# Decoding the retrieved experts of four token tiles together, with a binary selection of sub-keys

## The chip, the cores and the metric

The kernel runs on one core of a Trainium2 chip. The metric is the device time of one execution in microseconds (us), less being better. An execution varies by some 0.1% around the median.

## The reference, cut to what matters

A first block (attention with forget gates, RWKV-7 time mixing, gated feed-forward) and a second one (HGRN2, retention, a PEER feed-forward over 16384 experts) run over 512 tokens of width 1024. The change lies in the retrieval of PEER: for each token and each of 8 heads, the best 16 of 128 sub-keys are taken in each of two halves, the best 16 of their 256 sums follow, and each winner's position is turned back into an expert's index.

```python
q = (ht @ w_q).reshape(T, 8, 2, 128)
s = jnp.einsum('thpd,hpkd->thpk', q, sub_keys)
top_s, top_i = lax.top_k(s, 16)
cand = top_s[:, :, 0, :, None] + top_s[:, :, 1, None, :]
cand_idx = top_i[:, :, 0, :, None] * 128 + top_i[:, :, 1, None, :]
best_s, best_c = lax.top_k(cand.reshape(T, 8, 256), 16)
expert_idx = jnp.take_along_axis(cand_idx.reshape(T, 8, 256), best_c, axis=-1)
gates = jax.nn.softmax(best_s, axis=-1)
# out[t] = sum over the 128 winners e of gate * gelu(u_e . h_t) * v_e
```

## The kernel before

All weights stream through one ring in a fixed order. A tile `raw` of 128x1024 is loaded on SP's queue, ACT rounds it to `hi` (L245), and VectorE or POOL subtracts to get `lo` (L248); three matmuls (L271 to L273) then make one product of nearly full precision. While `pool_split` is 1 (from the start of `peer` to the end of the gate stage), all these subtractions are POOL's. `next_w` keeps three splits and five loads ahead. A scheduler that simulates the program sets the order of each engine's instructions from program order and priorities; on the chip each engine then works strictly in that order.

`peer` (L1423) does the last part of the second block. Its stages:

1. `retrieve` (L1239). For each of four pairs of heads `hp` and each of four halves `c`: a product with a piece of `w_q` (24 matmuls, L1255), a copy `q` on ACT (L1257), four matmuls with the sub-keys, one for each tile of 128 tokens (`psc`, L1260), a copy `sc` on ACT (L1262), and `top16` for each tile on VectorE (L1230: maximum of 8, their index, replacement, maximum, index). After two halves, POOL adds the candidates: of the 16x16 sums only those 112 are formed that can win, 4x16 and 12x4 (L1271, L1274), and `top16` takes 16 of the 112.
2. `decode` (L1281), once for each pair of heads and each tile, so 16 times. It makes the gates by softmax (the exponential is ACT's, L1288), turns a position among the 112 into two numbers from 0 to 15 by shifts, masks, casts and a predicated copy (L1297 to L1311), compares each with 0 to 15 (`eq`, 32x16 elements, L1313, VectorE), multiplies with the sub-key indices `tif` (L1314, POOL) and sums (`sel`, L1315, VectorE). The tiles go in the order 3, 0, 1, 2 and have buffers of their own.
3. `slots_T` (L1352): transposes of `sel` and the gates of the tiles 0 to 2, and a copy `slT` on ACT.
4. `gate_matrix` (L1363), the gate stage: in 96 groups of four tokens, one-hot tiles `ohA` (VectorE, four instructions, L1375) and `ohB` (three groups of eight on POOL, L1379, the others on VectorE, L1381), their products `pg` (L1384), and a copy to `gstage` (L1386), which goes to memory as a dense matrix of gates.
5. `expert_act` (L1390): products of the tokens with expert rows `u`, 24 matmuls of 384 columns and a GELU each. 40 of them stand ahead of the main loop: 25 without a condition, then 12 tied to finished gate groups, then 3 behind the last group.
6. The main loop over 128 groups of experts (L1452): `wf`, its split, and the products with `v`. Tile 3 goes another way here: its rows are gathered one by one (`gather_rows`, L1317) during that loop.

## Time and profile before

| | us |
|---|---|
| median of three runs | 3087.77 |
| the three runs | 3086.38 to 3088.63 |
| the profiled execution | 3085.74 |
| its span, first to last instruction | 3084.0 |
| TensorE busy, share of the span | 96% |
| VectorE, ACT, POOL busy | 63%, 40%, 49% |
| mean granted clock of TensorE | 0.986 |

The span is what the profiler recorded of one execution on the core. PE is TensorE's matmul row, PEld its weight loads, DVE is VectorE, SP the queue of transfers. Matmuls are pipelined, and a busy PE is not PE at its peak. The busy share is a mean over stages with different limits, so a stage is read by itself. The clock is given as a share of full speed.

### The profile page before, as it was taken

The page shows a single profiled execution, that of the slowest core. Times are in us where ns is not written, and L with a number is a line of the kernel's source. Part 1 is how long each engine was busy: PE and PEld are TensorE (multiplying, and loading weights), DVE is VectorE, ACT ScalarE, POOL GpSimd, SP SyncE. Part 2 cuts the span into 40 slices and gives each one's busy share as a digit, 9 for nine tenths or more (in the row PEclk, how much of TensorE's full clock was granted, in tenths as well). Part 3 has the DMA queues.
Part 4 walks back from the last instruction along what each step waited for, and adds up shares of the span by engine and source line. Part 5 has one row for each costly group of instructions (what it writes and reads, how often), then busy time and mean ns, then how long its engine had stood idle before and what let it go on. Part 6 is the DMA issues. An engine that isn't in the chain of part 4 may idle for free.

```text
span 3084.0 us, 40810 instructions
## 1 busy us (share of the span) xinstructions
PE 2945.5 (96%) x15129; PEld 2542.2 (82%) x15129; DVE 1940.8 (63%) x3421; ACT 1229.7 (40%) x1925; POOL 1507.6 (49%) x1150
## 2 busy tenths in 40 slices
PE   7998998999999999999999987888999999999998
PEld 6877787888878878888888877887899999999877
DVE  4247655443134663455532699999677878777898
ACT  5455654222242443344422323466333333333333
POOL 3213213222235662233332447877677777767775
PEclk9998999999999999999999998999999999999999
DMA  4120013333332112322233322345888888898897
GB/s 158 57 66 10 1 38 105 97 96 96 96 110 82 59 45 82 99 85 82 82 119 117 120 62 77 116 174 195 287 302 308 298 312 297 305 317 297 314 324 254
DMA packets 174358, 473.64 MB, mean 154 GB/s; under 512 B 15056, under 2 KB 64592, under 8 KB 172624
## 3 DMA queue, kind: packets, MB, share of 16 engines
q1 hardware_dynamic: 137296, 336.80, 33.4%
q0 software_dynamic: 36864, 134.23, 12.3%
q8 instruction: 120, 1.97, 0.3%
q14 instruction: 78, 0.64, 0.1%
HBM read 439.49 MB, written 31.46 MB: 153 GB/s over the span
## 4 chain that ended last, share of the span: by engine, by line
PE 77%; DVE 13%; issue 4%; DMA 2%; ACT 2%; POOL 2%; SPq 0%; DVEq 0%; POOLq 0%; ACTq 0%
PE acc L272 14%; PE acc L271 14%; PE acc L273 14%; PE A L273 3%; PE A L272 3%; PE A L271 3%; PE B L272 3%; PE B L271 3%; PE B L273 3%; PE pg L1384 2%; DMA urow<-ev,ei 2%; PE i L811 2%; PE lev L988 1%; DVE wk L1235 1%; PE C L273 1%
## 5 line engine op out<-in xcount | busy, mean ns | idle before, releaser
L248 POOL TENSOR_TENSOR lo<-raw,hi 128x1024 fp32r<-128x1024 f32 x224 | 553.0, 2470 | 758.2 <-ACT hi L245 729.1
L271 PE MATMUL acc<-u,hi 128*128 128x512 f32 (+3 forms) x2344 | 859.1, 367 | 16.9 <-ACT eact L1399 7.2
L273 PE MATMUL acc<-u,lo 128*128 128x512 f32 (+3 forms) x2344 | 859.3, 367 | 16.3 <-POOL lo L248 16.3
L272 PE MATMUL acc<-u,hi 128*128 128x512 f32 (+3 forms) x2344 | 858.6, 366 | 0.2 <-DVE u L478 0.2
L245 ACT ACTIVATE hi<-raw 128x1024 fp32r<-128x1024 f32 x447 | 472.5, 1057 | 944.2 <-PE acc L272 496.2
L248 DVE TENSOR_TENSOR lo<-raw,hi 128x1024 fp32r<-128x1024 f32 x223 | 318.2, 1427 | 297.3 <-ACT hi L245 297.0
L271 PEld LDWEIGHTS acc<-u,hi 128*128 128x128 f32 (+1 forms) x2344 | 444.9, 190 | 72.5 <-ACT eact L1399 8.5
L273 PEld LDWEIGHTS acc<-u,lo 128*128 128x128 f32 (+1 forms) x2344 | 444.9, 190 | 67.7 <-POOL lo L248 18.6
L272 PEld LDWEIGHTS acc<-u,hi 128*128 128x128 f32 (+1 forms) x2344 | 445.2, 190 | 54.1 <-issue 2.7
L1339 DVE SCALAR_TENSOR_TENSOR urow<-urow,h4row 128x1024 f32<-128x1024 f32 x128 | 198.4, 1557 | 92.1 <-DMA urow<-eu,ei 91.5
L1349 DVE SCALAR_TENSOR_TENSOR po<-urow,act,po 128x1024 f32<-128x1024 f32 x127 | 193.9, 1527 | 66.4 <-DMA urow<-ev,ei 65.6
L1331 POOL DMA_INDIRECT urow<-eu,ei x128 | 189.6, 1481 | 34.7 <-issue 22.8
L1331 POOL DMA_INDIRECT urow<-ev,ei x128 | 175.6, 1372 | 44.6 <-DVE po L1349 18.4
L1410 ACT ACTIVATE wh<-wf 128x384 fp32r<-128x384 f32 x128 | 67.2, 526 | 313.8 <-PE D L272 268.7
L248 POOL TENSOR_TENSOR lox<-rawx,hix 128x1024 fp32r<-128x1024 f32 x53 | 137.9, 2602 | 97.8 <-ACT hix L245 97.6
L1375 DVE TENSOR_SCALAR ohA<-iota,slT 128x128 f32<-128x128 f32 x384 | 129.7, 403 | 0.9 <-PE pg L1384 0.7
L1384 PE MATMUL pg<-ohB,ohA 128*128 128x128 f32 x768 | 106.0, 280 | 24.5 <-DVE ohB L1381 12.4
L1384 PEld LDWEIGHTS pg<-ohB,ohA 128*128 128x128 f32 x768 | 97.5, 191 | 31.9 <-ACT gstage L1386 17.2
L1386 ACT ACTIVATE gstage<-pg 128x512 f32<-128x512 f32 x96 | 99.4, 1091 | 57.0 <-PE pg L1384 57.0
L1379 POOL TENSOR_SCALAR ohB<-iota,slT 128x128 f32<-128x128 f32 x144 | 97.7, 696 | 39.9 <-PE pg L1384 39.8
L1411 DVE TENSOR_TENSOR wl<-wf,wh 128x384 fp32r<-128x384 f32 x128 | 101.4, 794 | 5.8 <-ACT wh L1410 4.1
L1407 DVE TENSOR_TENSOR wf<-eact,gread 128x384 f32<-128x384 f32 x98 | 69.0, 705 | 17.3 <-ACT eact L1399 16.2
(567 smaller groups left out, 5592.4 us busy)
## 6 DMA issues: line engine op xcount, KB each, us to landing
raw<-ut SPq DMA_DIRECT2D x128, 512.0 KB, 5.4
raw<-ev SPq DMA_DIRECT2D x75, 512.0 KB, 6.4
rawx<-ev SPq DMA_DIRECT2D x53, 512.0 KB, 7.0
raw<-w_ret SPq DMA_DIRECT2D x48, 512.0 KB, 3.6
gd<-gstage SPq DMA_DIRECT2D x12, 2048.0 KB, 7.0
gread<-gd SPq DMA_DIRECT2D x32, 768.0 KB, 8.9
raw<-w_gu SPq DMA_DIRECT2D x44, 512.0 KB, 3.6
raw<-w_hg SPq DMA_DIRECT2D x32, 512.0 KB, 3.6
```

Source lines behind the costliest of these rows:

```text
L245: self.nc.scalar.activation(hi, raw, AF.Copy)
L248: r = eng.tensor_tensor(lo, raw, hi.bitcast(F32), op=ALU.subtract)
L271: mm(out, a[0], b[0], start=start, stop=False)
L272: mm(out, a[0], b[1], start=False, stop=False)
L273: return mm(out, a[1], b[0], start=False, stop=stop).ins
L1331: r = nc.gpsimd.indirect_dma_start(out=u, out_offset=None, in_=src, in_offset=bass.IndirectOffsetOnAxis(ap=ei[:, s:s + 1], axis=0))
L1339: nc.vector.scalar_tensor_tensor(u, u, 1.0, row, op0=ALU.mult, op1=ALU.mult, accum_out=act[:, s:s + 1])
L1349: nc.vector.scalar_tensor_tensor(o, u, act[:, s:s + 1], o, op0=ALU.mult, op1=ALU.add)
L1375: nc.vector.tensor_scalar(A4[:, r], self.iota, sl[:, 0, k + r:k + r + 1], sl[:, 2, k + r:k + r + 1], op0=ALU.is_equal, op1=ALU.mult)
L1384: last = nc.tensor.matmul(p[:, r, :], A4[:, r], B4[:, r], start=True, stop=True)
L1386: nc.scalar.activation(st[:, :, q * 4:q * 4 + 4].rearrange("p j t -> p t j"), p, AF.Copy)
L1411: nc.vector.tensor_tensor(wl, wf, wh.bitcast(F32), op=ALU.subtract)
```

## The change

The four tiles of tokens get common tiles: `ts`, `ti`, `bs`, `bc`, `gate`, `sel` have a tile axis of 4. The candidate sums of all four tiles are two POOL instructions instead of eight. `decode` runs once for a pair of heads instead of four times. The comparison with 0 to 15, the product and the sum go; in their place the 16 sub-key indices are selected by the four bits of the position: ACT copies the lower eight indices to every slot (`mux`, 16x16x8 elements), and a predicated copy puts the upper eight over them where bit 3 is set; then the upper four over the lower four by bit 2, and so on down to one. The cast `tif` and the copies to `sel` are ACT's. The gates of tile 3 are copied to a tile of their own at the end.

```diff
-TILES = (3, 0, 1, 2)
...
-        self.gate = [self.b("gate3" if i >= NDENSE else "gate", [128, 8, 16]) for i in range(4)]
-        self.sel = [[self.b(f"sel{w}", [128, 8, 16]) for w in range(2)] for i in range(4)]
+        self.gate = self.b("gate", [128, 4, 8, 16])
+        self.sel = [self.b(f"sel{w}", [128, 4, 8, 16]) for w in range(2)]
         for hp in range(4):
-            ts = [self.b("ts", [128, 4, 16]) for i in range(4)]
-            ti = [self.b("ti", [128, 4, 16], U32) for i in range(4)]
-            bs = [self.b("bs", [128, 2, 16]) for i in range(4)]
-            bc = [self.b("bc", [128, 2, 16], U32) for i in range(4)]
+            ts, ti = self.b("ts", [128, 4, 4, 16]), self.b("ti", [128, 4, 4, 16], U32)
+            bs, bc = self.b("bs", [128, 4, 2, 16]), self.b("bc", [128, 4, 2, 16], U32)
...
-                for i in TILES:
-                    self.top16(ts[i][:, c, :], ti[i][:, c, :], s[:, i, :], 128)
+                for i in range(4):
+                    self.top16(ts[:, i, c, :], ti[:, i, c, :], s[:, i, :], 128)
                 if c % 2:


-                    for i in TILES:
-                        t0, t1 = ts[i][:, c - 1, :], ts[i][:, c, :]
-                        cand = self.b("cand", [128, 112])
-                        nc.gpsimd.tensor_tensor(cand[:, 0:64].rearrange("p (a b) -> p a b", b=16),
-                                                t0[:, 0:4, None].to_broadcast([128, 4, 16]),
-                                                t1[:, None, :].to_broadcast([128, 4, 16]), op=ALU.add)
-                        nc.gpsimd.tensor_tensor(cand[:, 64:112].rearrange("p (a b) -> p a b", b=4),
-                                                t0[:, 4:16, None].to_broadcast([128, 12, 4]),
-                                                t1[:, None, 0:4].to_broadcast([128, 12, 4]), op=ALU.add)
-                        self.top16(bs[i][:, c // 2, :], bc[i][:, c // 2, :], cand, 112)
-            for i in TILES:
-                self.decode(i, hp, ti[i], bs[i], bc[i])
-
-    def decode(self, i, hp, ti, bs, bc):
+                    t0, t1 = ts[:, :, c - 1, :], ts[:, :, c, :]
+                    cand = self.b("cand", [128, 4, 112])
+                    for o, a, nb in ((0, slice(0, 4), 16), (64, slice(4, 16), 4)):
+                        na = a.stop - a.start
+                        nc.gpsimd.tensor_tensor(cand[:, :, o:o + na * nb].rearrange("p i (a b) -> p i a b", b=nb),
+                                                t0[:, :, a, None].to_broadcast([128, 4, na, nb]),
+                                                t1[:, :, None, 0:nb].to_broadcast([128, 4, na, nb]), op=ALU.add)
+                    for i in range(4):
+                        self.top16(bs[:, i, c // 2, :], bc[:, i, c // 2, :], cand[:, i, :], 112)
+            self.decode(hp, ti, bs, bc)
+        self.gate3 = self.b("gate3", [128, 8, 16])
+        nc.scalar.activation(self.gate3, self.gate[:, 3], AF.Copy)
...
-        g = self.gate[i][:, H, :]
-        TT(g, bs, bs[:, :, 0:1].to_broadcast([128, 2, 16]), op=ALU.subtract)
+        g = self.gate[:, :, H, :]
+        B2 = [128, 4, 2, 16]
+        TT(g, bs, bs[:, :, :, 0:1].to_broadcast(B2), op=ALU.subtract)
         nc.scalar.activation(g, g, AF.Exp)
-        sm = self.t([128, 2], name="gsum")
+        sm = self.t([128, 4, 2], name="gsum")
         nc.vector.tensor_reduce(sm, g, axis=AX.X, op=ALU.add)
         nc.vector.reciprocal(sm, sm)
-        TT(g, g, sm[:, :, None].to_broadcast([128, 2, 16]), op=ALU.mult)
-        tif = self.b("tif", [128, 2, 2, 16])
-        nc.vector.tensor_copy(tif, ti.rearrange("p (h two) k -> p h two k", two=2))
-        B3, B4 = [128, 2, 16], [128, 2, 16, 16]
-        tail = self.b("cm", B3, U32)
+        TT(g, g, sm[:, :, :, None].to_broadcast(B2), op=ALU.mult)
+
+        ab = self.b("ab", [128, 4, 2, 2, 16], U32)
+        tail, u, f = self.b("cm", B2, U32), self.b("cu", B2, U32), self.b("cuf", B2)
         TS(tail, bc, 64, None, op0=ALU.is_ge)
-        for w in range(2):
-            uf = []
-            for n in range(2):
-                u = self.b("cu", B3, U32)
-                if w == 0:
-                    TS(u, bc, 4 - 2 * n, None, op0=ALU.logical_shift_right)
-                else:
-                    TS(u, bc, 15 - 12 * n, None, op0=ALU.bitwise_and)
-                f = self.b("cuf", B3)
-                nc.vector.tensor_copy(f, u)
-                uf.append(f)
-            if w == 0:
-                TS(uf[1], uf[1], -12.0, None, op0=ALU.add)
-            nc.vector.copy_predicated(uf[0], tail, uf[1])
-            eq = self.b("eq", B4)
-            TT(eq, uf[0][:, :, :, None].to_broadcast(B4), self.iota16[:, None, None, :].to_broadcast(B4), op=ALU.is_equal)
-            nc.gpsimd.tensor_tensor(eq, eq, tif[:, :, w, None, :].to_broadcast(B4), op=ALU.mult)
-            nc.vector.tensor_reduce(self.sel[i][w][:, H, :], eq, axis=AX.X, op=ALU.add)
+        TS(u, bc, 2, None, op0=ALU.logical_shift_right)
+        nc.vector.tensor_copy(f, u)
+        TS(f, f, -12.0, None, op0=ALU.add)
+        nc.vector.tensor_copy(u, f)
+        TS(ab[:, :, :, 0, :], bc, 4, None, op0=ALU.logical_shift_right)
+        nc.vector.copy_predicated(ab[:, :, :, 0, :], tail, u)
+        u = self.b("cu", B2, U32)
+        TS(u, bc, 3, None, op0=ALU.bitwise_and)
+        TS(ab[:, :, :, 1, :], bc, 15, None, op0=ALU.bitwise_and)
+        nc.vector.copy_predicated(ab[:, :, :, 1, :], tail, u)
+
+        tif = self.b("tif", [128, 16, 16])
+        nc.scalar.activation(tif, ti.rearrange("p i c k -> p (i c) k"), AF.Copy)
+        w = self.b("mux", [128, 16, 16, 8])
+        nc.scalar.activation(w, tif[:, :, None, 0:8].to_broadcast([128, 16, 16, 8]), AF.Copy)
+        n = 8
+        while n:
+            bit = self.b("bit", [128, 16, 16], U32)
+            TS(bit, ab.rearrange("p i h two k -> p (i h two) k"), n, None, op0=ALU.bitwise_and)
+            B4 = [128, 16, 16, n]
+            nc.vector.copy_predicated(w[:, :, :, 0:n], bit[:, :, :, None].to_broadcast(B4),
+                                      tif[:, :, None, 8:16].to_broadcast(B4) if n == 8 else w[:, :, :, n:2 * n])
+            n //= 2
+        w = w.rearrange("p (i h two) k e -> p i h two k e", h=2, two=2)
+        for j in range(2):
+            nc.scalar.activation(self.sel[j][:, :, H, :], w[:, :, :, j, :, 0], AF.Copy)
...
-        g, sel = self.gate[i], self.sel[i]
+        g = self.gate3
...
-        nc.vector.scalar_tensor_tensor(e, sel[0], 128.0, sel[1], op0=ALU.mult, op1=ALU.add)
+        nc.vector.scalar_tensor_tensor(e, self.sel[0][:, i], 128.0, self.sel[1][:, i], op0=ALU.mult, op1=ALU.add)
...
-        for w, a in enumerate((sel[0], sel[1], g)):
-            nc.tensor.transpose(p[:, w, :], a.rearrange("p a b -> p (a b)"), self.ident)
+        for w, a in enumerate((*self.sel, self.gate)):
+            nc.tensor.transpose(p[:, w, :], a[:, i].rearrange("p a b -> p (a b)"), self.ident)
...
-        P.open(eq1, "retrieve", "xs 10 gb keys q sc; eq 4 junk; ts 8; ti 8; bs 8; bc 8; wk 3; cand 3; tif 4; cm 4; cu 4; cuf 8; ef 1; gate 3; sel0 4; sel1 4")
+        P.open(eq1, "retrieve", "xs 10 gb keys q sc; mux 1; ts 2; ti 2; bs 2; bc 2; wk 3; cand 2; tif 1; ab 1; bit 2; cm 1; cu 2; cuf 1; ef 1; gate 1; sel0 1; sel1 1")
```

## Rows read from the trace of the kernel before

**Rows 1.** The page: busy us (share of the span) and instructions of each engine
```profile
PE 2945.5 (96%) x15129; PEld 2542.2 (82%) x15129; DVE 1940.8 (63%) x3421; ACT 1229.7 (40%) x1925; POOL 1507.6 (49%) x1150
```

**Rows 2.** Busy time by stretch: us, PE, PEld, DVE, ACT, POOL (instructions), clock, DMA
```profile
1727.00:1850.00 123.00, 110.02 (x579) 94.40 (x578) 113.34 (x611) 37.92 (x60) 58.56 (x58) 0.96 0.26 81
1850.00:1973.50 123.50, 96.57 (x491) 93.20 (x491) 122.81 (x503) 45.40 (x62) 88.91 (x74) 0.88 0.28 86
1973.50:2160.00 186.50, 162.02 (x1145) 154.75 (x1144) 178.65 (x445) 120.00 (x130) 140.53 (x162) 1.00 0.47 175
```

**Rows 3.** Groups on VectorE, 1737 to 1974 us: busy us, mean ns | idle before
```profile
L1313 DVE TENSOR_TENSOR eq<-cuf,iota 128x512 f32<-128x512 f32 x32 | 25.1, 817 | 0.0
...
L1311 DVE COPY_PREDICATED cuf<-cm,cuf 128x32 f32<-128x32 uint32 x32 | 16.6, 520 | 0.0
```

**Rows 4.** Timeline of VectorE: start us, us, instruction
```profile
1745.56 0.87 DVE L1232 MAX8 ts<-sc 128x8 f32<-128x128 f32 x4 [1.25 <-ACT sc L1262]
1746.35 0.07 DVE L1233 MATCH_VALUE_LOAD ti<-ts,sc 128x8 f32 x1
...
1746.86 0.08 DVE L1233 MATCH_VALUE_LOAD ti<-ts,sc 128x8 f32 x1
...
1836.23 0.34 DVE L1307 CAST cuf<-cu 128x32 f32<-128x32 uint32 x3
1836.49 0.17 DVE L1290 TENSOR_REDUCE gsum<-gate 128x2 f32<-128x32 f32 x1
...
1947.78 1.27 DVE L1313 TENSOR_TENSOR eq<-cuf,iota 128x512 f32<-128x512 f32 x2
1948.98 1.29 DVE L1310 TENSOR_SCALAR cuf<-cuf 128x32 f32<-128x32 f32 x1
...
1950.28 2.43 DVE L1311 COPY_PREDICATED cuf<-cm,cuf 128x32 f32<-128x32 uint32 x1
```

**Rows 5.** Groups on POOL, 1737 to 1974 us
```profile
L248 POOL TENSOR_TENSOR lo<-raw,hi 128x1024 fp32r<-128x1024 f32 x36 | 85.9, 2390 | 30.7 <-ACT hi L245 27.4 <-DMA raw<-w_q 3.3
L1314 POOL TENSOR_TENSOR eq<-eq,tif 128x512 f32<-128x512 f32 x32 | 46.8, 1476 | 31.9 <-DVE eq L1313 30.6 <-DVE gate L1292 1.4
```

**Rows 6.** Timeline of ACT
```profile
1750.22 1.06 ACT L245 ACTIVATE hi<-raw 128x1024 fp32r<-128x1024 f32 x1 [4.21 <-POOL cand L1271]
...
1756.59 1.06 ACT L245 ACTIVATE hi<-raw 128x1024 fp32r<-128x1024 f32 x1 [4.21 <-issue]
...
1833.86 0.57 ACT L1288 ACTIVATE gate<-gate 128x32 f32<-128x32 f32 x2 [12.31 <-DVE gate L1287]
...
1905.72 1.06 ACT L245 ACTIVATE hi<-raw 128x1024 fp32r<-128x1024 f32 x1 [2.73 <-POOL lo L248]
...
1909.88 1.06 ACT L245 ACTIVATE hi<-raw 128x1024 fp32r<-128x1024 f32 x1 [2.72 <-issue]
```

**Rows 7.** Waits, 1730 to 2250 us: us in total, times, longest
```profile
PE psc L1260 <- ACT q L1257: 8.7, 2, 8.5
```

**Rows 8.** One-hots of line 1375: ns min/median/max, first and last start us
```profile
L1375 DVE TENSOR_SCALAR ohA<-iota,slT x384: 331/338/2519, 1973.5 to 2159.0; 128x128 f32<-128x128 f32 x192
```

**Rows 9.** The chain that ended last, in order of time
```profile
1987.40 1.78 PE pg L1384 x16
```

**Rows 10.** The subtractions of line 248 by stretch: us, DVE, POOL, clock, DMA
```profile
1850.00:1973.50 123.50, 0.00 (x0) 48.35 (x21) 0.88 0.28 86
...
1982.00:2020.00 38.00, 0.00 (x0) 15.43 (x6) 1.00 0.41 139
...
2100.00:2140.00 40.00, 0.00 (x0) 4.73 (x2) 1.00 0.41 154
```

**Rows 11.** The copies of finished gate groups (line 1386) by stretch: us, ACT
```profile
1982.00:2020.00 38.00, 16.61 (x16) 1.00 0.41 139
...
2100.00:2140.00 40.00, 21.40 (x21) 1.00 0.41 154
```

**Rows 12.** Timeline at the start of the main loop
```profile
2175.59 1.03 DVE L1407 TENSOR_TENSOR wf<-eact,gread 128x384 f32<-128x384 f32 x2 [16.22 <-ACT eact L1399]
```

More of the change, by code (lines that the diff above doesn't have):

```diff
@@ L342, in consts @@
         ld(self.iota, I["io"])
-        self.iota16 = self.iota[:, 0:16]
         dv = cp.tile([128, 56], F32, name="dv")
@@ L1262, in retrieve, with decode @@
                 nc.scalar.activation(s, p, AF.Copy)
-                for i in TILES:
-                    self.top16(ts[i][:, c, :], ti[i][:, c, :], s[:, i, :], 128)
+                for i in range(4):
+                    self.top16(ts[:, i, c, :], ti[:, i, c, :], s[:, i, :], 128)
                 if c % 2:
-                    for i in TILES:
-                        t0, t1 = ts[i][:, c - 1, :], ts[i][:, c, :]
-                        cand = self.b("cand", [128, 112])
-                        nc.gpsimd.tensor_tensor(cand[:, 0:64].rearrange("p (a b) -> p a b", b=16),
-                                                t0[:, 0:4, None].to_broadcast([128, 4, 16]),
-                                                t1[:, None, :].to_broadcast([128, 4, 16]), op=ALU.add)
-                        nc.gpsimd.tensor_tensor(cand[:, 64:112].rearrange("p (a b) -> p a b", b=4),
-                                                t0[:, 4:16, None].to_broadcast([128, 12, 4]),
-                                                t1[:, None, 0:4].to_broadcast([128, 12, 4]), op=ALU.add)
-                        self.top16(bs[i][:, c // 2, :], bc[i][:, c // 2, :], cand, 112)
-            for i in TILES:
-                self.decode(i, hp, ti[i], bs[i], bc[i])
-    def decode(self, i, hp, ti, bs, bc):
+                    t0, t1 = ts[:, :, c - 1, :], ts[:, :, c, :]
[10 more added lines that the diff above has]
+        nc.scalar.activation(self.gate3, self.gate[:, 3], AF.Copy)
+    def decode(self, hp, ti, bs, bc):
         nc = self.nc
@@ L1354, in slots_T @@
         nc = self.nc
-        g, sel = self.gate[i], self.sel[i]
         p = self.b("pslT", [128, 3, 128])
-        for w, a in enumerate((sel[0], sel[1], g)):
-            nc.tensor.transpose(p[:, w, :], a.rearrange("p a b -> p (a b)"), self.ident)
+        for w, a in enumerate((*self.sel, self.gate)):
+            nc.tensor.transpose(p[:, w, :], a[:, i].rearrange("p a b -> p (a b)"), self.ident)
         t_ = self.B([128, 3, 128], f"slT{i}", 1)
```

## The prediction

> **What bounds the kernel now.** I read the page first, then its slices, then only the stretch that the diff touches. TensorE is busy for 96% of the span [rows 1], so a saving counts only where TensorE is held up. The table of stretches shows where that is [rows 2]: in the retrieval (1727 to 1973.5 us) and in the gate stage behind it (to 2160 us) VectorE is the full engine (113, 123 and 179 us of 123, 123.5 and 186.5), and TensorE is the one with gaps, 40 us of idle time and a granted clock of 0.96 and 0.88 in the retrieval. From 2175.6 us, when the first `wf` runs [rows 12], the main expert loop is TensorE's; whatever ends earlier before it moves the end by as much.
>
> VectorE's line of work in the retrieval runs without a gap from the first MAX8 at 1745.6 us [rows 4] to the first one-hot at 1973.5 us [rows 8]: 228 us. The one-hots need `slT`, `slT` needs the last decode. So the retrieval lasts as long as VectorE's instructions do, and the gate stage (96 groups of four tokens) is again VectorE's.
>
> TensorE's own work is the floor. A weight split of the query products comes every 6.37 us, one of the expert products every 4.16 us [rows 6], and 16 `pg` records, two groups, take 1.78 us of the chain [rows 9]. That is 16 x 6.37 = 102, 40 x 4.16 = 166 and 48 x 1.78 = 85 us, 353 us in all: from 1727 us it could reach the expert loop at 2080 us, not 2175.6. TensorE therefore limits a saving only beyond 95 us.
>
> **What the decode costs now.** Durations of neighbours overlap on VectorE, so I take spacing from start to start [rows 4]: four MAX8 take 0.79 us (0.20 each), an index pass with a replace pass 0.51, so a selection of 16 from 128 (maximum, index and replace, maximum, index) costs 0.20 + 0.51 + 0.20 + 0.26 = 1.17 us. 64 of these are 75 us. The 32 selections from 112 candidates have no long row here; scaled by width, 0.9 x 1.17, they are 34 us. Selections stay, at 109 us. The decode is the remainder: 228 - 109 = 119 us.
>
> What it consists of matters, since only part is arithmetic. 32 one-hot compares and 32 reductions of 512 elements at 0.60 us (two compares fill 1.20) are 38 us; 272 instructions of at most 64 elements at 0.086 us (three casts fill 0.26) are 23 us. That is 61. The other 58 us are waits inside instructions: a predicated copy of 32 elements took 2.43 us and averages 0.52, an add of -12 on as many took 1.29, and the 512-element compare averages 0.82 us where two undisturbed ones end after 1.27 [rows 3, 4]. Such a stall has the length of one of POOL's subtractions, 2.39 us [rows 5]; MAX8, index, replace and reduction do not show it.
>
> **What it costs afterwards.** For each pair of heads one decode handles all four tiles. It has 14 small instructions, 13 of them of 128 elements (the reciprocal has 8); no row has this width here without a stall. Between 32 elements (0.086) and 512 (0.60) the slope is 1.07 ns an element, so 128 cost 0.19 us: 2.5 us. Four bit tests of 256 elements at 0.33: 1.3 us. Four predicated copies of 2048, 1024, 512 and 256 elements at the same slope: 4.3 us. Together 8.1 us, four times: 32 us. From below: the 32-element cast and the compare bound a wide one-source instruction poorly; at half the slope all of it is 18 us. From above: a predicated copy that needs two passes adds 4 x 4 us, 48 in all. I take 32, since the 512-element compare, with two broadcast inputs, is the nearest kind.
>
> The product `eq x tif` leaves POOL (47 us [rows 5]), and `sel` and `tif` move to ACT. ACT's added work is four broadcasts of 2048 elements, about 2.1 us each (twice the 1.06 us of a 1024-element copy [rows 6]), and a dozen short copies; ACT is under half busy there [rows 2], so this is free while nothing waits behind it (the last rival).
>
> Stalls: 58 us now fall on about 40 us of instructions that can stall (compares 19, small ones 21), with POOL's subtractions and products busy 133 of 228 us. Afterwards the instructions that can stall are some 32 us and POOL's work is about 30 subtractions x 2.39 = 72 us in a retrieval of some 170 us. By stall for instruction time, scaled by busy over free time of POOL (1.4 before, 0.73 after), that gives 58 x 32/40 x 0.73/1.4 = 24; I take 22. The bounds are one half subtraction for each decode, 5 us, and the stalls of now scaled by POOL's time alone, 58 x 72/133 = 31.
>
> New waits of VectorE: the candidates of a pair now wait for all four tiles and are two POOL instructions of 256 and 192 elements, at most the 1.48 us of 512 [rows 5], possibly behind a subtraction: up to 3.6 us, eight times. Seven have the next selections or the previous decode queued as cover; the last has none. At the end, after the last predicated copy, come `sel` on ACT, three transposes, `slT`, and only then the first one-hot; before, VectorE still had other tiles to decode meanwhile. About 3.5 us of short steps. I take 7 us; bounds 3.6 and 8 x 3.6 + 7 = 36.
>
> The moved products: Between 1850 and 1973.5 us POOL subtracted for 21 expert products, one every 5.9 us [rows 10]. A retrieval shorter by 58 us lets it do some 8 fewer before the one-hots start (at the present pace 10; at TensorE's own 4.16 us with no more holds, 15 or 16 fit into what is left, 5 or 6 fewer). They then run beside the one-hots, where the split costs VectorE: 38 us with six subtractions hold 16 groups, while 40 us later with two hold 21 [rows 10, 11]; the median one-hot takes 0.34 us, the longest 2.52 [rows 8]. One subtraction costs about its 2.4 us. Eight are 19 us; five are 12; if they stay behind the last group, eight cost 33 us of TensorE. I take 20.
>
> Sum: 119 - 32 - 22 - 7 - 20 = 38 us. The profiled execution took 3085.7 us (span 3084.0, the rest lies around it), 2 us under the median of 3087.8. Forecast: **3048 us**. The bounds all at once give 3006 and 3115.
>
> **A rule beside the rows.** A stalled copy lasts 2.43 us where a POOL subtraction lasts 2.39 [rows 4, 5]; whether a long VectorE instruction holds POOL up in the same way, these rows don't say. The Trainium skill, "SBUF — State Buffer", section "SBUF: two separate sides", says that VectorE and GpSimd hold a shared pair of ports for a whole instruction, and that an instruction with two SBUF inputs takes part. By it the predicated copies of up to 2.2 us would lock POOL out as well, which speaks against the change: the sum by the rows is 38 us, by that rule at its full price 21. This trace has no long predicated copy to test it.
>
> **Rivals.**
> - *More is saved (3013 us).* The wide instructions run at half the slope, decodes meet few subtractions, and the products fit: 119 - 18 - 10 - 4 - 14 = 73. For it: TensorE's floor leaves 95 us. Against: the compare of 512 shows no such speed.
> - *Most is given back behind the retrieval (3065 to 3078 us).* The long copies, 4 x 4.3 = 17 us, keep POOL from subtracting, the products come that much later: 3065. If the moved ones also run behind the last group on TensorE (33 instead of 20 us), 3078. For it: the gate stage already slows where subtractions are dense. Against: POOL loses 47 us of products and has room. The skill's page above states the lock on which this rests.
> - *No change.* The gains and the waits cancel near 3086, with eight uncovered candidate waits (36) and two-pass copies (48): 119 - 48 - 22 - 36 - 20 = -7.
> - *Slower (about 3116 us).* ACT works in order. Each decode now puts an exponential and two `sel` copies that wait for VectorE ahead of the next weight splits. ACT already lost 12.3 us before one exponential [rows 6], and TensorE 8.5 us before one `psc` for want of `q` [rows 7]. Two blocks a decode, eight of 8.5 us, are 68 us against the 38: 30 us slower. It decides from 4.8 us a block. Against: TensorE has three split weights in hand, and of sixteen exponentials only a few held it that long.
>
> **Chances.** Forecast (3030 to 3066) 0.56; more saved 0.16; mostly given back 0.14; no change 0.05; slower 0.09. About 0.2% (6 us) can be told from no change here: faster 0.86, same 0.05, slower 0.09. The range 3018 to 3076 cuts the ends of the second and third cases and leaves out the last two, some 0.2.
>
> **What would show it.** First one-hot 165 to 175 us after the first MAX8 (now 228); predicated copies of 2048 elements near 2.2 us when undisturbed; no POOL product; fewer expert products before the first one-hot and a gate stage of 195 to 210 us; first `wf` near 2138. It is wrong if VectorE shows long idle before candidates or one-hots, or if TensorE waits for `lo` or `q` through the retrieval.

## The result and the profile after

The changed kernel takes 3051.97 us (median of four runs, 3048.74 to 3052.76) against 3088.2 us before (3086.38 to 3090.75): a ratio of 0.988, with a 95% interval of 0.9863 to 0.9897. The forecast was 3048 us, its range 3018 to 3076.

The page of the profile after, busy us and instructions of each engine, beside [rows 1]:

```profile
PE 2937.2 (96%) x15129; PEld 2539.3 (83%) x15129; DVE 1868.9 (61%) x3173; ACT 1230.8 (40%) x1924; POOL 1456.4 (48%) x1070
```

VectorE has 248 instructions and 72 us less, POOL 80 instructions and 51 us less; TensorE has the same number. The span is 3049.5 us (3084.0 before). Where the 35 us come from is in the stretches, with the columns of [rows 2]; the last two divide the gate stage where its character changes:

```profile
1727.00:1850.00 123.00, 112.81 (x600) 98.03 (x600) 110.96 (x607) 45.26 (x66) 49.45 (x28) 0.96 0.28 84
1850.00:1912.20 62.20, 50.14 (x269) 49.03 (x269) 60.05 (x261) 27.78 (x38) 34.82 (x18) 0.91 0.33 99
1912.20:2126.00 213.80, 198.66 (x1373) 194.02 (x1373) 176.35 (x444) 133.59 (x148) 157.05 (x170) 0.99 0.48 173
1920.00:2040.00 120.00, 120.00 (x826) 119.96 (x826) 89.01 (x217) 74.03 (x85) 91.58 (x92) 1.00 0.50 171
2040.00:2126.00 86.00, 70.86 (x514) 66.29 (x513) 79.57 (x213) 57.74 (x60) 61.70 (x78) 1.00 0.48 184
```

Read the second line first: the retrieval ends at 1912.2 us instead of 1973.5, 61 us earlier, and in the whole of it (the first two lines) TensorE stands idle for 10 + 12 us, not 40. Then the third: this stretch, the gate stage, is 213.8 us long where it was 186.5, and TensorE is busy for 198.7 us of it, not 162. The longer retrieval had held products that now run in the gate stage. From 1727 us to the first `wf`, the start of the main loop, the same columns read, before and after:

```profile
1727.00:2175.60 448.60, 383.16 (x2294) 356.43 (x2293) 414.81 (x1557) 210.11 (x258) 295.58 (x296) 0.95 0.37 128
```

```profile
1727.00:2139.50 412.50, 374.07 (x2310) 353.21 (x2310) 347.40 (x1311) 212.09 (x259) 248.47 (x217) 0.97 0.41 139
```

TensorE has the same work there (the counts differ by records that are missing from a trace), and its idle time falls from 65 to 38 us: in the retrieval from 40 to 22, in the rest from 25 to 16. Its busy time falls from 383 to 374 us; the granted clock's shortfall (0.05 x 449 = 22 us before, 0.03 x 412 = 12 after, an estimate) would account for that. TensorE's longest wait in the retrieval of before, for POOL's `lo`, is not among its waits in the kernel after:

```profile
PE acc L273 <- POOL lo L248: 16.3, 6, 5.5
```

The main loop starts at 2139.47 against 2175.59 us [rows 12], 36 us earlier:

```profile
1742.04 0.88 DVE L1230 MAX8 ts<-sc 128x8 f32<-128x128 f32 x4 [5.09 <-ACT sc L1259]
...
1786.81 2.46 DVE L1315 COPY_PREDICATED mux<-bit,tif 128x2048 f32<-128x2048 uint32 x1
...
1871.00 4.49 DVE L1315 COPY_PREDICATED mux<-bit,tif 128x2048 f32<-128x2048 uint32 x1
...
1907.22 2.49 DVE L1315 COPY_PREDICATED mux<-bit,mux 128x512 f32<-128x512 uint32 x2
...
1912.23 2.52 DVE L1379 TENSOR_SCALAR ohA<-iota,slT 128x128 f32<-128x128 f32 x4 [1.15 <-ACT slT L1364]
...
2139.47 1.03 DVE L1411 TENSOR_TENSOR wf<-eact,gread 128x384 f32<-128x384 f32 x2 [16.04 <-DMA gread<-gd]
```

This timeline of VectorE after (start, duration) shows the retrieval's ends: first MAX8 at 1742.0 us, first one-hot at 1912.2, 170 us. The first MAX8 of before ran at 1739.3 us, ahead of the line of work that the prediction counts from 1745.6 [rows 4].

VectorE's groups in that stretch (busy us, mean ns | idle before), the new decode's largest:

```profile
L1315 DVE COPY_PREDICATED mux<-bit,tif 128x2048 f32<-128x2048 uint32 x4 | 13.9, 3466 | 0.0
L1315 DVE COPY_PREDICATED mux<-bit,mux 128x1024 f32<-128x1024 uint32 x4 | 10.1, 2513 | 0.0
L1313 DVE TENSOR_SCALAR bit<-ab 128x256 uint32<-128x256 uint32 x16 | 8.5, 557 | 0.0
```

The waits, 1730 to 2150 us (total, times, longest):

```profile
POOL cand L1269 <- DVE ts L1234: 40.4, 13, 12.3
ACT sel L1320 <- DVE mux L1315: 38.1, 4, 11.9
...
DVE ohB L1385 <- PE pg L1388: 33.5, 23, 7.3
...
ACT tif L1307 <- DVE ti L1235: 16.2, 4, 7.8
...
PE psc L1257 <- ACT q L1254: 10.2, 4, 5.5
...
PE acc L270 <- ACT x L1403: 8.6, 2, 7.1
...
PE pslT L1362 <- ACT sel L1320: 3.5, 1, 3.5
...
DVE bs L1230 <- POOL cand L1269: 0.7, 2, 0.3
```

Four readings: VectorE hardly waits for the new candidates (0.7 us in all); ACT does wait long before `sel`; TensorE's 22 us of idle time in the retrieval are waits for ACT (10.2 for `q`, 8.6 for the GELU that frees an accumulator, 3.5 for `sel`); and in the gate stage VectorE, which was the full engine there, now waits 33.5 us for TensorE's `pg`.

### The profile page after: what moved, and what is told of

The parts are those of the page before. It is cut to its first block, busy times and chain, and to the rows that moved or that the text cites. A ratio compares the mean times of both kernels' runs of the same rounds, so it can differ in the third digit from the quotient of the medians.

```text
span 3049.5 us, 40450 instructions
## 1 busy us (share of the span) xinstructions
PE 2937.2 (96%) x15129; PEld 2539.3 (83%) x15129; DVE 1868.9 (61%) x3173; ACT 1230.8 (40%) x1924; POOL 1456.4 (48%) x1070
## 4 chain that ended last, share of the span: by engine, by line
PE 63%; DVE 8%; issue 5%; DMA 4%; POOL 3%; ACT 1%; POOLq 0%; DVEq 0%; SPq 0%; ACTq 0%
PE acc L270 12%; PE acc L271 12%; PE acc L272 12%; DMA urow<-ev,ei 3%; PE A L272 3%; PE A L271 3%; PE A L270 3%; PE B L271 3%; PE B L270 3%; PE B L272 3%; PE pg L1388 2%; POOL urow L1336 1%; PE lev L986 1%; DVE mux L1315 1%; DVE wk L1233 1%
## 5 line engine op out<-in xcount | busy, mean ns | idle before, releaser
L247 DVE TENSOR_TENSOR lo<-raw,hi 128x1024 fp32r<-128x1024 f32 x223 | 311.6, 1398 | 297.4 <-ACT hi L244 297.1
L1354 DVE SCALAR_TENSOR_TENSOR po<-urow,act,po 128x1024 f32<-128x1024 f32 x127 | 200.8, 1581 | 71.7 <-DMA urow<-ev,ei 70.6
L1379 DVE TENSOR_SCALAR ohA<-iota,slT 128x128 f32<-128x128 f32 x384 | 117.4, 371 | 2.3 <-ACT slT L1364 1.1
L1385 DVE TENSOR_TENSOR ohB<-iota,slT 128x512 f32<-128x512 f32 x60 | 66.4, 1107 | 33.7 <-PE pg L1388 33.5
```

The source lines that it names most:

```text
L247: r = eng.tensor_tensor(lo, raw, hi.bitcast(F32), op=ALU.subtract)
L1354: nc.vector.scalar_tensor_tensor(o, u, act[:, s:s + 1], o, op0=ALU.mult, op1=ALU.add)
L1379: nc.vector.tensor_scalar(A4[:, r], self.iota, sl[:, 0, k + r:k + r + 1], sl[:, 2, k + r:k + r + 1], op0=ALU.is_equal, op1=ALU.mult)
```

## The experiments

Twelve kernels, each timed against the kernel before on the same chip (its median there: 3087.0 to 3089.0 us). All times are us; the first four columns come from the profiled execution, the products are counted by their GELUs, the last gate group by the start of its copy on ACT. Between profiled executions of different kernels the main loop alone differs by about 3 us either way, so a few microseconds of a median are read together with the first `wf`. Single executions spread more than the 0.1% said above: those of the kernel before on one chip lay between 3084.15 and 3095.95 us. A product counts as run when its GELU starts; 40 run in all, the last three of them behind the last gate group.

| kernel | first one-hot | products before it | one-hot to last group | first wf | median | ratio, 95% |
|---|---|---|---|---|---|---|
| before | 1973.5 | 21 | 187.5 | 2175.6 | 3088.2 | |
| after | 1912.2 | 12 | 212.8 | 2139.5 | 3051.97 | 0.9863 to 0.9897 |
| 1 no matmuls of seven | 1914.4 | 10 real | 203.6 | 2133.8 | 3044.43 | 0.9841 to 0.9874 |
| 2 no splits of seven | 1906.7 | 12 | 212.9 | 2134.0 | 3046.67 | 0.9843 to 0.9881 |
| 3 sel on VectorE | 1917.5 | 12 | 213.3 | 2145.0 | 3052.49 | 0.987 to 0.9903 |
| 4 batch, old selection | 1939.4 | 21 | 186.8 | 2140.3 | 3052.74 | 0.9873 to 0.9906 |
| 5 binary, tile by tile | 1945.7 | 15 | 201.3 | 2161.7 | 3067.76 | 0.9919 to 0.9955 |
| 6 longest copy twice | 1925.9 | 14 | 205.6 | 2146.3 | 3052.31 | 0.9866 to 0.9899 |
| 7 twenty ahead | 1911.2 | 13 | 211.8 | 2137.7 | 3051.43 | 0.9862 to 0.9898 |
| 8 products evened | 1914.3 | 12 | 209.5 | 2138.4 | 3047.51 | 0.9848 to 0.9881 |
| 9 neither, of seven | 1915.1 | 12 | 196.2 | 2127.8 | 3035.45 | 0.9818 to 0.9845 |
| 10 splits on VectorE | 1915.5 | 14 | 196.0 | 2126.0 | 3036.06 | 0.9823 to 0.985 |
| 11 the same, evened | 1919.2 | 14 | 198.0 | 2130.2 | 3034.78 | 0.9818 to 0.9845 |
| 12 kernel 4 and 10 | 1944.4 | 23 | 168.0 | 2126.6 | 3036.06 | 0.9815 to 0.9842 |

**What the moved products cost.** The prediction charged them to VectorE, 2.4 us of stall each. The rival is TensorE: their matmuls fill it. Kernel 1 takes only the matmuls of seven products away, kernel 2 only their weight loads and splits.

```diff
-        for k in range(8):
+        for k in range(0 if 10 <= j < 17 else 8):
...
+        if 10 <= j < 17:
+            p = hi.bitcast(F32)
```

> The changed kernel with seven of the early expert products (10 to 16) robbed of their 24 matmuls; their weights are still loaded and split, and the GELU reads the split weights instead of a product, so the activations of those seven experts groups are not the reference's. Theory T (the products that the shorter retrieval pushes into the gate stage cost TensorE's time, 4.16 us each): 7 x 4.16 = 29 us less, 3023 us. Theory V (they cost VectorE, which POOL's subtractions stall, 2.4 us each): the subtractions are all still there, so within 5 us of 3052.

```diff
-        hi, lo = self.next_w()
+        skip = 10 <= j < 17
+        hi, lo = (None, None) if skip else self.next_w()
...
+            w = (H4[k][0][:, q], H4[k][1][:, q]) if skip else (hi[:, s], lo[:, s])
...
-        P.want([U_(j) for j in range(NFIFO)])
+        P.want([U_(j) for j in range(NFIFO) if not 10 <= j < 17])
```

> The changed kernel with the same seven products keeping their matmuls, but on blocks of the token matrix instead of weights, so that seven loads and seven splits on ACT and POOL are gone (those seven activations are not the reference's). Theory T: TensorE's time is unchanged, so 3052 us within 5. Theory V: seven subtractions fewer beside the one-hots, 7 x 2.4 = 17 us less, 3035 us.

Each gives little: 7.5 and 5.3 us by the median (the intervals in the table overlap with that of the kernel after), 5.7 and 5.5 by the first `wf`. Of the seven products two, 10 and 11, lie ahead of the one-hots in the kernel after and five in its gate stage, so the stage of kernel 1 has 20 real products instead of 25. Without these matmuls it is 9.2 us shorter, 1.8 us for each of the five. Without their splits it is not shorter at all (212.9 against 212.8 us); kernel 2's gain comes from a retrieval that ends 5.5 us earlier. What the missing matmuls left in the retrieval of kernel 1 became a wait of the transposes on TensorE for `sel`, 18.6 us instead of 3.5:

```profile
PE pslT L1362 <- ACT sel L1320: 18.6, 1, 18.6
```

So in the gate stage a product's split alone costs nothing that shows, and its matmuls cost less than half of the 4.16 us that TensorE takes for them. Kernel 9 takes both away from seven products, all of them in the gate stage.

```diff
+        if 13 <= j < 20:
+            a = self.b("eact", [128, n])
+            self.nc.scalar.activation(a, H4[0][0].bitcast(F32)[:, :n], AF.Gelu_apprx_tanh)
+            return a
...
-        P.want([U_(j) for j in range(NFIFO)])
+        P.want([U_(j) for j in range(NFIFO) if not 13 <= j < 20])
```

> The changed kernel without the expert products 13 to 19, all of which stand in its gate stage: no load, no split, no matmul; a GELU of a token tile fills their place, so those seven activations are not the reference's. Taking only the matmuls or only the splits from seven products (partly ahead of the one-hots) was worth 5 to 8 us. Theory F (in the gate stage TensorE and VectorE are both nearly full, VectorE by its stalls under POOL's subtractions, so only taking both shows a product's price): 7 x 2.0 to 2.8 us, 3032 to 3038 us. Rival (a fixed order or a chain of transfers sets the end of the gate stage): 3048 to 3053 us.

That gives 16.5 us by the median and 11.7 by the first `wf`, 1.7 to 2.4 us a product; the gate stage is 16.6 us shorter, 2.4 us for each of seven. Kernel 1's 1.8 us is for five products in the stage, so the medians (16.5 against 7.5 and 5.3) must not be compared as they stand: most of a product's price is in its matmuls, and only the difference of some 0.6 us, from one profiled execution of each kernel, may be a part that shows when both go. Where the price arises is in two views of the kernel after. The subtractions of line 247 by stretch (us, DVE, POOL, clock, DMA), beside [rows 10]:

```profile
1920.00:2040.00 120.00, 0.00 (x0) 43.75 (x20) 1.00 0.50 171
2040.00:2126.00 86.00, 0.00 (x0) 13.94 (x6) 1.00 0.48 184
```

And the copies of finished groups (us, ACT), beside [rows 11]:

```profile
1920.00:2040.00 120.00, 47.56 (x46) 1.00 0.50 171
2040.00:2126.00 86.00, 51.30 (x50) 1.00 0.48 184
```

With 20 subtractions, 120 us hold 46 groups, and there TensorE is busy for 120.00 us of 120 and VectorE for 89. With six, 86 us hold 50 groups, and VectorE is the full one (79.6). TensorE's prices come close to the first part: 46 groups at 0.89 and 20 products at 4.16 us are 124 us. The moved products have made the crowded part longer, in which TensorE is the full engine, and the part behind it is still VectorE's, with its stalls.

Kernel 10 leaves all the work in and moves the subtractions from product 12 on from POOL to VectorE, until the main loop:

```diff
+            if j == 10:
+                self.pool_split = 0
```

> The changed kernel with the subtractions for the products from number 12 on done by VectorE instead of POOL until the end of the gate stage (1.22 us each there, no stall of 2.4). Theory V (the stalls are VectorE's price in the gate stage): VectorE needs 96 x 1.42 + 25 x 1.22 = 167 us instead of 196, TensorE's 189 us then set the stage: 195 to 200 us instead of 213, 3035 to 3042 us. Theory T (TensorE alone is the limit there): 3049 to 3055 us.

It is 15.9 us faster by the median, 13.5 by the first `wf`, though VectorE, the full engine of the second part, gets 24 subtractions more in the stage. VectorE's groups from 1900 to 2170 us, first of the kernel after, then of kernel 10:

```profile
L1379 DVE TENSOR_SCALAR ohA<-iota,slT 128x128 f32<-128x128 f32 x384 | 117.4, 371 | 2.3 <-ACT slT L1364 1.1 <-PE pg L1388 0.7
L1385 DVE TENSOR_TENSOR ohB<-iota,slT 128x512 f32<-128x512 f32 x60 | 66.4, 1107 | 33.7 <-PE pg L1388 33.5
```

```profile
L1379 DVE TENSOR_SCALAR ohA<-iota,slT 128x128 f32<-128x128 f32 x384 | 112.6, 360 | 1.1 <-PE pg L1388 0.6
L247 DVE TENSOR_TENSOR lo<-raw,hi 128x1024 fp32r<-128x1024 f32 x36 | 47.5, 1320 | 24.6 <-ACT hi L244 24.6
L1385 DVE TENSOR_TENSOR ohB<-iota,slT 128x512 f32<-128x512 f32 x60 | 41.1, 684 | 11.4 <-PE pg L1388 11.4
```

The 60 `ohB` take 41 us instead of 66 and the longest `ohA` falls from 2521 to 470 ns, as these two views of all one-hots show (min/median/max), after and kernel 10:

```profile
L1379 DVE TENSOR_SCALAR ohA<-iota,slT x384: 332/339/2521, 1912.2 to 2123.1; 128x128 f32<-128x128 f32 x192
```

```profile
L1379 DVE TENSOR_SCALAR ohA<-iota,slT x384: 332/342/470, 1915.5 to 2109.5; 128x128 f32<-128x128 f32 x192
```

A subtraction costs VectorE 1.32 us as its own work and up to about 2.2 (2521 less 339 ns) as a stall under POOL's. So the stall is a price that can be avoided; the matmuls can't be. But not all of the gain is shown to be the stall. The gate stage and the time to the first `wf` in kernel 10:

```profile
1915.50:2112.00 196.50, 186.56 (x1316) 182.39 (x1315) 171.73 (x468) 130.29 (x143) 98.23 (x140) 1.00 0.50 183
```

```profile
1727.00:2126.00 399.00, 369.60 (x2312) 349.51 (x2312) 347.83 (x1341) 212.19 (x258) 180.12 (x187) 0.98 0.43 144
```

VectorE's busy time in the stage is 172 us with these subtractions and was 176 without them. TensorE's idle time there falls from 15 to 10 us, but it also has 57 matmuls fewer in the stage: two more products run ahead of the one-hots (14 instead of 12) in the order of this kernel. Over both stages TensorE's idle time falls from 38 to 29 us. That POOL, with fewer subtractions, delivers its own `ohB` sooner is not the cause: TensorE waits for these 2.2 us in the stage, against 1.7 in the kernel after, and for VectorE's `ohB` 3.8 us against 7.7. How much of the 13.5 us the two products give and how much the stalls, no run separates.

**Evening the products out.** Kernel 8 lowers the number of products that the order asks for early, so that they spread over both halves of the gate stage; kernel 11 does so on top of kernel 10.

```diff
-NEARLY, NLATE, NLAG = 25, 3, 10
+NEARLY, NLATE, NLAG = 13, 3, 10
```

> The changed kernel with NEARLY 13 instead of 25: the 24 products from number 13 on are spread evenly over the 96 gate groups, one for four groups, where now 13 crowd ahead of the groups and then one comes for eight. Theory F (in the crowded part TensorE is full and VectorE waits for it, in the thin part VectorE is full and TensorE waits, so evening it out gives both work): four groups and a product are 7.7 us on TensorE and about 8 on VectorE, the gate stage 195 to 200 us instead of 213, total 3037 to 3043 us. Theory V (each product costs VectorE its 2 to 2.4 us stall wherever it stands): 3049 to 3055 us.

> As the run before, and with the products spread evenly over the gate groups (NEARLY 13). Theory F (both engines were full, each in its part): TensorE has 7.7 us of work for four groups and a product, VectorE some 7, so the stage comes near TensorE's 189 us: 190 to 196 us, 3030 to 3036 us. Rival (evening out adds nothing to it): as the run before.

Kernel 8 is 4.5 us faster by the median, 1.1 by the first `wf`: no more than these runs can tell, and between the two forecasts. Kernel 11 stands with kernel 10. Spreading the products is worth little; in a window of 20 us of kernel 8 both engines are nearly full at once:

```profile
2000.00:2020.00 20.00, 19.00 (x138) 18.81 (x137) 19.78 (x45) 12.36 (x14) 13.79 (x16) 1.00 0.61 224
```

**ACT's order.** The waits above fit the rival that ACT, in order, holds up the splits behind its `sel` copies: 38.1 us in four. Kernel 3 puts the copies on VectorE.

```diff
-            nc.scalar.activation(self.sel[j][:, :, H, :], w[:, :, :, j, :, 0], AF.Copy)
+            nc.vector.tensor_copy(self.sel[j][:, :, H, :], w[:, :, :, j, :, 0])
```

> The changed kernel with the eight copies to sel on VectorE instead of ACT. Theory A (ACT, held 38 us in four waits for the last predicated copy, keeps back weight splits, and TensorE lies idle some 22 us in the retrieval for it): three to five more products fit into the retrieval, 12 to 20 us less, 3032 to 3040 us. Rival (the held ACT costs nothing, since VectorE sets the end of the retrieval): eight more VectorE copies of about 0.2 us, 3052 to 3055 us.

Nothing is gained: 3052.49 us, twelve products ahead again, and the first `wf` 5.5 us later. But ACT isn't freed by it either. What it doesn't wait before `sel` it waits in part before the next decode's `tif`, 34.7 us instead of 16.2:

```profile
ACT tif L1307 <- DVE ti L1235: 34.7, 4, 13.3
```

So ACT's hold before `sel` has no price that this kernel shows. Whether ACT's order costs some of the 22 us that TensorE waits for ACT in the retrieval stays open.

**The two halves of the change.** Kernel 4 decodes four tiles at once with the old selection (equality with 16 indices, POOL's product, a reduction); kernel 5 keeps the decode and the candidate sums tile by tile, as before, and selects by bits (both cut, against the kernel after).

```diff
+            TT(eq, uf[0][:, :, :, None].to_broadcast(B4), self.iota[:, None, None, 0:16].to_broadcast(B4), op=ALU.is_equal)
+            nc.gpsimd.tensor_tensor(eq, eq, tif[:, :, w, None, :].to_broadcast(B4), op=ALU.mult)
+            m = self.b("msel", B3)
+            nc.vector.tensor_reduce(m, eq, axis=AX.X, op=ALU.add)
```

> Batching alone: the four tiles are decoded together as in the changed kernel, but a sub-key is selected as before, by comparing with 0 to 15 (now 2048 elements on VectorE), product on POOL, sum on VectorE. Theory B (both halves of the change are needed; the small instructions and their stalls shrink, but 38 us of compares and sums stay and the products of 2048 elements still run on POOL): retrieval 20 to 35 us shorter than before, of which some 0.6 arrives, 3066 to 3076 us. Rival (the gain is all from fewer instructions that can stall): 3052 us. Rival (it is all from the selection): 3088 us.

```diff
-            self.decode(hp, ti, bs, bc)
+            for i in TILES:
+                self.decode(i, hp, ti[i], bs[i], bc[i])
...
-            B4 = [128, 16, 16, n]
+            B4 = [128, 4, 16, n]
```

> The binary selection alone: one decode for each tile and pair of heads as before, in the order 3, 0, 1, 2, but with the predicated copies of the changed kernel, a quarter as wide. Arithmetic 48 us instead of 61 (small ones 19, bit tests 10, copies 19), no product on POOL, but 352 short VectorE instructions that can stall. Theory B (either half shortens the retrieval by some 25 to 35 us, and with as many products ahead of the one-hots that arrives): 3053 to 3064 us. Rival (without batching the stalls stay and eat it): 3075 to 3088 us.

Batching alone gives all of it: 3052.74 us. Selection by bits alone gives about 20 us (0.9937), between its two forecasts. Kernel 4's stretches (columns as above), the last from 1727 us to the first `wf`:

```profile
1727.00:1850.00 123.00, 116.30 (x622) 102.16 (x621) 111.82 (x584) 40.72 (x62) 64.75 (x31) 0.97 0.31 90
1850.00:1939.40 89.40, 84.14 (x467) 83.12 (x467) 73.24 (x278) 35.59 (x52) 74.18 (x31) 0.96 0.37 110
1939.40:2127.00 187.60, 161.11 (x1138) 153.16 (x1137) 173.23 (x445) 120.66 (x130) 134.16 (x160) 1.00 0.47 173
1727.00:2140.30 413.30, 373.80 (x2293) 350.37 (x2292) 358.29 (x1304) 202.53 (x250) 280.25 (x224) 0.98 0.41 138
```

Its first one-hot comes at 1939.4 us, 27 us later than in the kernel after, but TensorE is idle for only 12 us of the retrieval, 21 products are done by then, and the gate stage is as short as before. By the first `wf` the two differ by 0.8 us, and TensorE's idle time up to there is 39.5 us in the one and 38.4 in the other. On top of kernel 10's edit (made here nine steps of the loop later, since more products stand ahead: now 23, where kernel 10 has 14) it is the same:

```diff
+            if j == 19:
+                self.pool_split = 0
```

> Batching with the old comparison and sum (first one-hot at 1939 us, 21 products ahead of it), and the subtractions for the gate stage's products on VectorE. It asks whether the binary selection, which brings the first one-hot 27 us forward and moves nine products behind it, is worth more once a moved product no longer stalls VectorE. If the 2.4 us stall was the price of a moved product: the 16 products of this kernel's gate stage gain 16 x 1 us or so, 3037 to 3043 us, and the binary selection is then worth up to 7 us. If TensorE's total alone decides now: 3033 to 3037 us, as with the binary selection.

Kernel 12: 3036.06 us, kernel 10: 3036.06 us.

**A longer retrieval, and more products ahead.** Kernel 6 runs the longest predicated copy twice; kernel 7 asks for twenty products ahead of the transposes.

```diff
+            for _ in range(2 if n == 8 else 1):
+                nc.vector.copy_predicated(w[:, :, :, 0:n], bit[:, :, :, None].to_broadcast(B4),
...
```

> The changed kernel with the predicated copy of 2048 elements made twice in each decode (the second changes nothing): four copies of 2.35 us more on VectorE, the retrieval 9 to 12 us longer. Theory F (behind the retrieval TensorE is the full engine; what the retrieval loses, the gate stage gains, since TensorE's products move): at most 4 us more, 3050 to 3056 us. Rival R (the end of the retrieval is on the path in full): 3061 to 3065 us.

```diff
+        for j in range(20):
+            acts[j] = self.expert_act(H4, j)
...
-        for j in range(NEARLY):
+        for j in range(20, NEARLY):
```

> The changed kernel with 20 expert products put ahead of the transposes for slT in program order instead of the 12 that the scheduler put there: the first one-hot comes some 30 us later, at 1940 to 1948 us, and the gate stage holds 17 products instead of 25. Theory F: 3048 to 3056 us, as now. Rival R (an earlier first one-hot is worth most of its time): 33 us later, less eight products at 2 us, 3069 us.

In kernel 6 the first one-hot is 13.7 us later, two more products stand ahead of it, the gate stage is 7.2 us shorter; the first `wf` is 6.8 us later and the median 0.3 us: half of the delay, or by the median all of it, is gone at the end. Kernel 7 tells nothing: the order that was computed for TensorE still put 13 products ahead, so what was to be changed was not changed.

## Why the prediction was right

**Removed and added decode, with its stalls.** Forecast 119 us out, 32 + 22 in. Added up from start to start over the trace's records of VectorE, the selections take 111 us before and after (forecast 109), and the decode 121 us before and 55 after, against 54. Inside the 55 two sizes were off and cancelled. The copies cost more than 4.3 us a decode: undisturbed the four take 2.44, 1.24, 1.27 and 1.25 us (the timeline of kernel 6 at the end of this text), 6.2, so 8 us more in all. Stalls cost less: about 15 us, if the copies' 25 and 15 for the bit tests and small instructions, at the forecast's prices (4 x 3.8), are taken from the 55. (The forecast's lower bound, 18 us "at half the slope", is 20 by its own rows; the sum doesn't rest on it.)

**The 2048-element copies** were to take 2.2 us undisturbed; one above took 2.46, and another 4.49 when POOL subtracted beside it.

**POOL held up by long copies.** POOL's subtractions in the retrieval, a group of the kernel after, beside the 2390 ns of [rows 5], and then POOL's timeline beside the copies that began at 1786.81 and 1871.00 us:

```profile
L247 POOL TENSOR_TENSOR lo<-raw,hi 128x1024 fp32r<-128x1024 f32 x28 | 74.1, 2653 | 59.7 <-ACT hi L244 56.4 <-DMA raw<-w_q 3.3
```

```profile
1786.97 2.74 POOL L1269 TENSOR_TENSOR cand<-ts 128x256 f32<-128x256 f32 x1 [4.81 <-DVE ts L1234]
...
1870.73 6.98 POOL L247 TENSOR_TENSOR lo<-raw,hi 128x1024 fp32r<-128x1024 f32 x2
...
1873.10 4.62 POOL L247 TENSOR_TENSOR lo<-raw,hi 128x1024 fp32r<-128x1024 f32 x1
```

Each lengthens the other: a candidate addition of 256 elements, whose mean is 0.63 us in kernel 4, took 2.74 under the first copy. Of the two subtractions beside the second copy the one that had begun before it took its usual 2.4 us (6.98 for both, the last line is the second of them alone), the copy took 2.0 us more than undisturbed, and the subtraction that began under the copy took 4.62. The Trainium skill, "SBUF — State Buffer", section "SBUF: two separate sides", says that the two engines share a pair of ports, held for a whole instruction; these rows agree: what began first kept its length, and the other lasted about until the first had ended and its own length more. As a price it stayed small, 28 x 0.26 = 7 us on POOL, which was idle for 60 us before these instructions. The rival that rests on it did not come about.

**New waits of VectorE.** Forecast 7 us: measured 4.5, of which 0.7 for the candidates, 1.3 for later scores, and 2.5 from the last copy to the first one-hot.

**The moved products.** Forecast: eight fewer ahead of the one-hots, 20 us. Measured: nine fewer (21 to 12), a gate stage 25 us longer. The number nearly held, but not the reason that was given, a price of VectorE's, one subtraction's 2.4 us each. [Rows 10] and [rows 11] were read as if VectorE set the pace where subtractions are dense. In the same 38 us of the kernel before TensorE was busy throughout:

```profile
1982.00:2020.00 38.00, 38.00 (x266) 38.00 (x266) 36.23 (x81) 23.85 (x28) 31.79 (x30) 1.00 0.41 139
```

In the gate stage of the kernel after, five splits fewer change nothing (kernel 2), the matmuls of five products fewer give 1.8 us each (kernel 1), and both fewer give 2.4 us for each of seven (kernel 9). So it is mainly TensorE's work that moved, and that its price lies near the length of a subtraction is luck. VectorE's stalls do cost time in the part behind it, as kernel 10 suggests, but they are not the price of the products that moved. The forecast of 195 to 210 us for the gate stage was a little short of 213. The prediction's bound "TensorE limits only beyond 95 us" counts TensorE's work as if it could be spread at will. The order doesn't spread it: what isn't done in the retrieval is done at the front of the gate stage. The bound is also too wide: instead of 353 us TensorE was busy for 383 before and 374 after, which left 65 us of idle time before, not 95.

**The sum.** 61 - 25 = 36 us at the first `wf`, 36.2 us in the medians; forecast 38 from the profiled execution, 40 from the median. But the path that the sum follows, VectorE's line through the retrieval less the moved products, is not the only one to this time: kernel 4 reaches it with a retrieval only 34 us shorter and no product moved. What the kernels have in common is TensorE's idle time up to the first `wf`: 65 us before, 38 after and 39 in kernel 4.

**The rivals.** ACT's order did not cost what that rival asked, eight blocks of 8.5 us: TensorE's `psc` waited 10.2 us in all for `q`, against 8.7 [rows 7]. A smaller price is not ruled out, since kernel 3 doesn't free ACT. "More is saved" needed the copies at half the slope, and the products to fit; neither was so. Its 3013 us would not have come from a faster decode either: kernels 4, 6 and 12 show that, once the tiles are batched, an earlier end of the retrieval is handed back by the gate stage, by half (kernel 6) or nearly all of it (kernel 4 against the kernel after, 12 against 10). Batching is enough for the 36 us; on top of it the selection by bits adds nothing that these runs can tell from zero, and without it some 20 us.

**Better than both:** kernels 10 to 12, 3035 to 3036 us, 16 us under the changed kernel and 52 under the one before; kernel 12 reaches it with the old selection, kernel 10 with the new.

Left open: whether more products could run ahead of the one-hots in the kernel after (kernel 7 did not bring it about; TensorE's 22 us of idle time there would hold five), why the order on TensorE puts nine fewer ahead when the decode gets shorter, and by what step batching takes away TensorE's idle time.

## What to carry to other kernels

Before counting a stage's saving, list what other engines did under it: here 61 us of a stage's own path became 36 because nine products that it had covered moved to the next stage. Count the idle time of the engine that has the most work over both stages: it doesn't change when work only moves. A stage that loses its long pole may not have one bound but two in turn: look at it in windows, and take away one engine's work, the other's, and both, from the same number of items in the same stage. Where VectorE is stalled for 2 us by an elementwise instruction of POOL that VectorE itself does in 1.3, moving it to VectorE can be faster although VectorE is the full engine.

## What was not expected of the hardware

Predicated copies stop shrinking with their size where they run in strided rows (stretches of neighbouring elements under one predicate) of four elements or fewer. Kernel 6's timeline of VectorE, one copy of each size that no subtraction of POOL's touched:

```profile
1787.42 2.44 DVE L1316 COPY_PREDICATED mux<-bit,tif 128x2048 f32<-128x2048 uint32 x1
...
1797.39 1.24 DVE L1316 COPY_PREDICATED mux<-bit,mux 128x1024 f32<-128x1024 uint32 x1
...
1800.49 1.27 DVE L1316 COPY_PREDICATED mux<-bit,mux 128x512 f32<-128x512 uint32 x1
...
1803.05 1.25 DVE L1316 COPY_PREDICATED mux<-bit,mux 128x256 f32<-128x256 uint32 x1
```

All copies of kernel 5, with a quarter of the rows (min/median/max ns):

```profile
L1316 DVE COPY_PREDICATED mux<-bit,mux x48: 400/422/2595, 1790.3 to 1944.4; 128x256 f32<-128x256 uint32 x16, 128x128 f32<-128x128 uint32 x16, 128x64 f32<-128x64 uint32 x16
L1316 DVE COPY_PREDICATED mux<-bit,tif x16: 708/732/2006, 1786.7 to 1940.4; 128x512 f32<-128x512 uint32 x16
```

With 256 rows in a partition, 1024, 512 and 256 elements (four, two and one a row) all take about 1.25 us, where the forecast had 1.15, 0.6 and 0.33; with 64 rows, 256, 128 and 64 elements have a median of 0.42. From the difference, (1.25 - 0.42) us over 192 rows, a row of up to four elements costs some 4.3 ns, an estimate. Eight a row take about twice that, 2.44 us. So the last two steps of the selection by bits, with 768 elements, cost together as much as the first with 2048.
